# The opening of a two-block transformer kernel: condition, x, modulation tiles and first weights

## The chip, the cores and the metric

The kernel runs on one core of a Trainium2 chip, as one program. The metric is the device time of an execution in microseconds (us); of several runs the median stands. A profile is one execution with the hardware profiler on; its span runs from the first to the last instruction.

## The reference

Two transformer blocks of two layers each work on 256 tokens of 1024 features, in float32. Only the beginning of the first block matters here. A condition vector `c` of 1024 numbers goes through Silu and a matrix of 1024 x 6144 per layer, which gives shifts, scales and gates; the normed tokens are scaled and shifted with them and multiplied by the input weights.

```python
c_act = jax.nn.silu(c)
...
mod = c_act @ w_ada[l] + b_ada[l]
sh1, sc1, gt1, sh2, sc2, gt2 = jnp.split(mod, 6, axis=-1)
h = modulate(rms_norm(x, norm_mix[l]), sh1, sc1)
p = h @ w_in[l]
```

`modulate` is h * (1 + scale) + shift. Behind p come a dilated attention, an RWKV-7 recurrence and a gated MLP, a merge, a convolutional feed-forward network, the second layer, and then the second block.

## The kernel before

Activations lie feature-major: a tensor of 1024 x 256 is eight tiles of 128 x 256 (blocks k = 0 to 7). Every weight matmul is done three times to keep float32 accuracy: `wload` (L125) loads halves of 128 x 1024 float32, ACT casts each to a rounded `hi` (L137), VectorE takes the rest as `lo` (L138), `split` (L195) does the same to activations as `h` and `l` (L201, L202), and `mm3` (L162) multiplies hi by h, hi by l and lo by h (L164 to L166).

The opening, in `build` (L1319), runs in this order of the program. SP's queue loads the identity, the condition as one row `crow`, the eight tiles of x (L1328, 128 KB each), and two pairs of columns of `w_in` (12 and 6, in two halves each). ACT applies Silu to the row; TensorE copies it to all partitions with a matmul of ones, and ACT evacuates that to `cact` (L1344, L1345). `LayerA` (L345) then goes through the 16 modulation tiles of the first 2048 outputs. A tile f is 128 outputs x 1024 inputs, 512 KB. Tiles 0 to 7 make the shifts, 8 to 15 the scales of blocks 0 to 7. They come in pairs of 1 MB, in the order of j = 0, 4, 1, 5, 2, 6, 3, 7 (f = 2j and 2j + 1), the last two pairs in halves; the third weight pair (`late`, columns 10) is loaded ahead of those halves. For each tile VectorE multiplies by `cact` and sums along the row (L371) into one column of `mods`.

`mod_cols` (L389) adds biases and makes `sh` and `am` for two blocks at a time (L396 to L398), so two blocks need four tiles. `modulated` (L412) takes the norm's factor from `rms`: squares on ACT (L215), a running sum on VectorE (L222), matmuls with a column of ones (L228), a root on ACT and a reciprocal (L240, L241), and a spread over all partitions (`spread`, L248). It then multiplies (L418), scales and shifts on ACT (L419), and splits. `mix_a` (L733) starts with `fmulti` (L175): three weight pairs, two columns of outputs each, over the eight blocks, 144 matmuls. The three second columns take banks of a pool of two (`aux`), so one of them waits for an evacuation (L434, L435). The first matmul behind the group is that with the `lora` weights (L467).

A scheduler puts each engine's instructions in order ahead of time, by their place in the program and by when it expects their operands; each engine then keeps its order. `keep_in_program_order` ties an instruction behind the one traced before it on its engine. Eight semaphores go round among the transfers, so an issue waits until the transfer eight places ahead has landed.

Of the kernel before, what the change touches and what calls it, by code (L numbers as in the profile page):

```python
# [17 lines left out]
S = 256  # L18
# [4 lines left out]
C1 = -0.5 * math.exp(-0.5)  # L23
ADA_EVERY = 0.67
PTAPS = 7
FILL = {("f", 0): ((0, 0), (0, 1)), ("f", 1): ((1, 0), (1, 1))}
PBANKS = (4, 2, 2)
PACE = (0.8, 1.5)
# [22 lines left out]
class K:  # L51
    def __init__(self, tc, ctx, ins):
        self.tc, self.nc, self.ins = tc, tc.nc, ins
        E = ctx.enter_context
        self.const = E(tc.tile_pool(name="const", bufs=1))
        self.xp = E(tc.tile_pool(name="xp", bufs=9))
        self.hp = E(tc.tile_pool(name="hp", bufs=17))
        self.wk = E(tc.tile_pool(name="wk", bufs=5))
        self.pm = E(tc.tile_pool(name="pm", bufs=PBANKS[0], space=PSUM))
        self.pa = E(tc.tile_pool(name="pa", bufs=PBANKS[1], space=PSUM))  # L60
        self.pr = E(tc.tile_pool(name="pr", bufs=PBANKS[2], space=PSUM))
        self.dr = E(tc.tile_pool(name="dr", bufs=1, space=DRAM))
        self.n = 0
        self.bg = []
        self.pj = {}
        self.due = 0.0
        self.wps = []
        self.turn = {"raw": 0, "split": 0}
        nc = self.nc
        self.ones = self.const.tile([128, 128], F32, name="ones")  # L70
        nc.vector.memset(self.ones, 1.0 / D)
        self.cols = {}
        self.ca = self.const.tile([128, NCA], F32, name="ca")
# [157 lines left out]
    def rms(self, x, spread=True, tail=False, both=False):  # L231
# [2 lines left out]
        b = self.spread(r, spread)  # L234
        return (r, b) if both else b

    def inv_rms(self, ms):
        nc = self.nc
        r = self.wk.tile([128, 4], F32, tag="st", name=self.nm("rc"), bufs=4)[:, :2]
        nc.scalar.activation(r, ms, AF.Sqrt, bias=self.k(1e-6))  # L240
        nc.vector.reciprocal(r, r)  # L241
        return r
# [83 lines left out]
def v3(t, a):  # L326
    return t.rearrange("p (a b) -> p a b", a=a)
# [14 lines left out]
class LayerA:  # L342


    def __init__(self, G, l, pool, cact, first=None, late=None):  # L345
        nc = G.nc
        self.G, self.l = G, l
        self.pool = p = pool
# [7 lines left out]
        if first is None:  # L356
            self.load_small()
        else:

            for n, j in enumerate((0, 4, 1, 5, 2, 6, 3, 7)):  # L360
                if n == 6:
                    late()
                raw = first.tile([128, 2, D], F32, tag="ada", bufs=8, name=G.nm("raw"))
                src = v3(G.ins["w_ada"][l, j], 2)
                if n < 6:
                    nc.sync.dma_start(raw, src)
                for h in range(2):
                    if n >= 6:
                        nc.sync.dma_start(raw[:, h, :], src[:, h, :])
                    f = 2 * j + h  # L370
                    nc.vector.scalar_tensor_tensor(raw[:, h, :], raw[:, h, :], 1.0, cact, MUL, MUL, accum_out=self.mods[f // 8][:, f % 8:f % 8 + 1])  # L371
        G.bg += [((l, f), ada_task(G, l, f, self.mods, cact)) for f in range(0 if first is None else 16, 48)]

    def load_small(self):
# [36 lines left out]

def modulated(G, x, a, sh):  # L412
    nc = G.nc
    r = G.rms(x, False, True)
    out = []
    for k in range(8):
        t = G.tmp(S)
        nc.vector.tensor_tensor(t, x[k], r, MUL)  # L418
        nc.scalar.activation(t, t, AF.Identity, scale=a[:, k:k + 1], bias=sh[:, k:k + 1])  # L419
        out.append(G.split(t))  # L420
    return out
# [893 lines left out]
def build(tc, ins, outs, stages="AB", depth=DEPTH, dbg=None):  # L1315
    with ExitStack() as ctx:
# [2 lines left out]
        nc = G.nc  # L1319
        G.weights(ctx.enter_context(tc.tile_pool(name="wpa", bufs=1)), 3, 4)  # L1320
        x = []
        G.load_ident()
        LB = nf = sk = pre = None

        def load_x():
            for k in range(8):
                t = G.x1()
                nc.sync.dma_start(t, ins["x"][:, k, :])  # L1328
                x.append(t)
        if "A" in stages:  # L1330
            with tc.tile_pool(name="la", bufs=2) as lp, tc.tile_pool(name="lc", bufs=1) as lc:
# [4 lines left out]
                    pre.append(G.wload(ins["w_in"][0, i], 2048))  # L1336
                with tc.tile_pool(name="st", bufs=1) as sp:
                    G.weights(sp, 3, 2)
                    crow = sp.tile([1, D], F32, name="crow")
                    nc.sync.dma_start(crow, ins["c"])  # L1340
                    nc.scalar.activation(crow, crow, AF.Silu)
                    for i in range(2):
                        ps = G.aux()
                        nc.tensor.matmul(ps, G.ones[0:1, :], crow[:, i * 512:i * 512 + 512], start=True, stop=True)  # L1344
                        nc.scalar.activation(cact[:, i * 512:i * 512 + 512], ps, AF.Copy, scale=float(D))  # L1345
                    load_x()
                    load_w(12)
                    load_w(6)
                    L = [LayerA(G, 0, lp, cact, sp, lambda: load_w(10))]
                    G.wps.pop()  # L1350
                L[0].load_small()
                G.load_consts()
                for l in range(depth):
# [3 lines left out]
                    with tc.tile_pool(name=f"fa{l}", bufs=1) as mp, tc.tile_pool(name=f"wxa{l}", bufs=1) as wx:  # L1357
# [13 lines left out]
                        x = ffn_a(G, L[l], x, l, mp, hook)  # L1371
                        G.wps.pop()
        else:
            load_x()
            G.load_consts()
            with tc.tile_pool(name="la", bufs=1) as lp:
# [129 lines left out]
def arrays(**i):  # L1506
# [2 lines left out]
    out = {"ca": _consts(), "onehot": _onehot()}  # L1509
    out["x"] = _tok(i["x"][0])  # L1510
    out["c"] = i["c"]
    out["w_ada"] = np.ascontiguousarray(i["w_ada"].reshape(L, D, 24, 2, 128).transpose(0, 2, 4, 3, 1)).reshape(L, 24, 128, 2048)
    cw = i["ffn_conv_w"]
    va = [_feat(v) for v in (i["norm_mix"], i["norm_ffn"], i["rwkv_mu"], i["rwkv_w0"], i["rwkv_a0"], i["rwkv_k_k"], i["rwkv_k_a"],
# [59 lines left out]
```

## Time and profile before

| what | value |
|---|---|
| median of 3 runs | 2295.76 us (2294.28 to 2296.1) |
| the profiled execution's own time | 2297.13 us |
| its span | 2295.3 us |
| mean granted TensorE clock | 0.990 |
| TensorE busy | 2206.4 us |
| VectorE (DVE) busy | 1685.2 us |
| ScalarE (ACT) busy | 1286.4 us |
| read from HBM | 408.40 MB |

In the profile PE is TensorE's matmuls and PEld its weight loads, DVE is VectorE, SPq and ACTq are the queues of SyncE and ScalarE. A matmul of plain float32 appears as two records of PE. "L371" is line 371 of the kernel. In brackets stands how long an engine was idle and what ended that.

### The profile page before, as it was taken

Reading aid. Unit: us, or ns where it says so; the run is one execution under the profiler, and the core shown is the slowest. Engines: PE = TensorE matmul, PEld = TensorE weight load, DVE = VectorE, ACT = ScalarE, POOL = GpSimd, SP = SyncE. Lnnn points to the kernel's source line nnn. Section 1 sums busy time; section 2 is a strip of 40 time slices with the busy share of each in tenths; the row PEclk is TensorE's granted clock in tenths of the full one; section 3 lists DMA queues with packets and bytes.
Section 4 is the critical chain, followed back from the end, with each engine's and each line's share of the span. In section 5 each row is a group of like instructions: output and inputs, shape, how many; then the busy total and the mean of one; then the engine's idle time right before and its main releaser. Section 6 shows DMA issues by size and latency. Waiting matters only on the chain.

```text
span 2295.3 us, 46372 instructions
## 1 busy us (share of the span) xinstructions
PE 2206.4 (96%) x18850; PEld 2131.8 (93%) x18850; DVE 1685.2 (73%) x3042; ACT 1286.4 (56%) x2184; POOL 4.2 (0%) x10
## 2 busy tenths in 40 slices
PE   5999998978999999999999999999999999999999
PEld 4889998978888999899999999999999999999999
DVE  6887777757678877776576569976677656997665
ACT  4575546544557554655454466664465446665444
POOL 0000000000000000000000000000000000000000
PEclk9999999989999999999999999999999999999999
DMA  7634457777563446765675663466565556346653
GB/s 289 200 121 150 148 192 256 224 220 231 179 188 122 150 150 190 262 213 156 176 238 170 173 196 109 140 216 184 158 209 182 171 175 194 102 149 214 184 159 124
DMA packets 129148, 416.66 MB, mean 182 GB/s; under 512 B 14596, under 2 KB 20356, under 8 KB 128166
## 3 DMA queue, kind: packets, MB, share of 16 engines
q1 hardware_dynamic: 126750, 409.50, 57.0%
q10 hardware_dynamic: 2184, 4.19, 1.0%
q8 instruction: 148, 2.42, 0.4%
q14 instruction: 66, 0.54, 0.1%
HBM read 408.40 MB, written 5.24 MB: 180 GB/s over the span
## 4 chain that ended last, share of the span: by engine, by line
PE 77%; DMA 9%; DVE 7%; ACT 5%; issue 1%; SPq 0%; ACTq 0%; DVEq 0%
PE ps L164 22%; PE ps L165 22%; PE ps L166 22%; DVE lo L138 3%; DMA skew<-ohb 2%; ACT hi L137 2%; DMA raw<-in_ffn_up 2%; DMA raw<-in_w_ada 2%; DMA raw<-in_w_in 1%; PE rec L601 1%; PE rec L593 1%; DVE raw L371 1%; DMA raw<-in_w_out 1%; PE rec L1182 1%; PE aux L1044 0%
## 5 line engine op out<-in xcount | busy, mean ns | idle before, releaser
L164 PE MATMUL ps<-h,hi 128*128 128x256 f32 x5080 | 1437.1, 284 | 31.0 <-ACT h L201 28.5
L166 PE MATMUL ps<-h,lo 128*128 128x256 f32 x5080 | 1433.2, 283 | 15.4 <-DVE lo L138 15.4
L165 PE MATMUL ps<-l,hi 128*128 128x256 f32 x5080 | 1432.2, 283 | 5.1 <-DVE l L202 5.0
L137 ACT CAST hi<-raw 128x1024 fp32r<-128x1024 f32 (+1 forms) x724 | 704.8, 977 | 640.2 <-PE ps L165 360.3
L138 DVE TENSOR_TENSOR lo<-raw,hi 128x1024 fp32r<-128x1024 f32 (+1 forms) x724 | 819.7, 1134 | 300.7 <-ACT hi L137 297.6
L164 PEld LDWEIGHTS ps<-h,hi 128*128 128x128 f32 x5080 | 959.7, 189 | 44.1 <-ACT h L201 30.8
L166 PEld LDWEIGHTS ps<-h,lo 128*128 128x128 f32 x5080 | 961.2, 189 | 21.0 <-DVE lo L138 16.8
L165 PEld LDWEIGHTS ps<-l,hi 128*128 128x128 f32 x5080 | 961.2, 189 | 11.2 <-DVE l L202 6.8
L201 ACT CAST h<-t 128x256 fp32r<-128x256 f32 x172 | 68.7, 403 | 126.1 <-DVE t L1000 96.2
L202 DVE TENSOR_TENSOR l<-t,h 128x256 fp32r<-128x256 f32 x172 | 72.5, 424 | 66.1 <-ACT h L201 65.7
L338 DVE SCALAR_TENSOR_TENSOR raw<-raw,cact 128x1024 f32<-128x1024 f32 x80 | 97.4, 1218 | 30.3 <-DMA raw<-in_w_ada 30.2
L997 DVE TENSOR_TENSOR t<-ps,r 128x512 f32<-128x512 f32 x88 | 60.8, 691 | 41.6 <-PE ps L166 41.2
L1187 DVE SCALAR_TENSOR_TENSOR cy<-cp,cwh,cy 128x256 f32<-128x256 f32 x192 | 85.2, 478 | 3.2 <-ACT cy L1185 2.9
L215 ACT ACTIVATE t<-x 128x256 f32<-128x256 f32 x96 | 38.5, 407 | 16.4 <-DVE x L968 9.1
L222 DVE TENSOR_TENSOR t<-t,t 128x256 f32<-128x256 f32 x87 | 36.6, 421 | 5.4 <-ACT t L215 4.1
L190 PE MATMUL ps<-hi,h 128*128 128x256 f32 x128 | 38.2, 299 | 0.0
L191 PE MATMUL ps<-hi,l 128*128 128x256 f32 x128 | 37.7, 294 | 0.0
L1000 DVE TENSOR_TENSOR t<-t,t 128x256 f32<-128x256 f32 x88 | 36.9, 420 | 1.0 <-ACT t L999 1.0
L192 PE MATMUL ps<-lo,h 128*128 128x256 f32 x128 | 37.4, 292 | 0.0
L999 ACT ACTIVATE t<-t 128x256 f32<-128x256 f32 x88 | 36.1, 411 | 0.9
L964 ACT ACTIVATE t<-t 128x256 f32<-128x256 f32 x44 | 18.1, 415 | 27.3 <-DVE t L963 27.0
L419 ACT ACTIVATE t<-t,sh,am 128x256 f32<-128x256 f32 x32 | 18.1, 596 | 26.5 <-DVE am L398 22.5
(312 smaller groups left out, 1890.3 us busy)
## 6 DMA issues: line engine op xcount, KB each, us to landing
raw<-in_w_in SPq DMA_DIRECT2D x176, 512.0 KB, 4.3
raw<-in_ffn_in SPq DMA_DIRECT2D x176, 512.0 KB, 4.5
raw<-in_ffn_up SPq DMA_DIRECT2D x88, 512.0 KB, 5.6
raw<-in_w_ada SPq DMA_DIRECT2D x84, 512.0 KB, 4.8
raw<-in_ffn_out SPq DMA_DIRECT2D x64, 384.0 KB, 3.1
raw<-in_ffn_out SPq DMA_DIRECT2D x64, 320.0 KB, 3.2
raw<-in_w_branch SPq DMA_DIRECT2D x24, 512.0 KB, 4.2
raw<-in_ffn_down SPq DMA_DIRECT2D x32, 384.0 KB, 3.1
```

Of the source, the lines that this page charges most:

```text
L137: nc.scalar.copy(hi[:, :m], raw[:, :m])
L138: nc.vector.tensor_tensor(lo[:, :m], raw[:, :m], hi[:, :m], SUB)
L164: mm(ps, w[0], x[0], start=first, stop=False)
L165: mm(ps, w[0], x[1], start=False, stop=False)
L166: mm(ps, w[1], x[0], start=False, stop=last)
L190: mm(ps[:, :256], x[k][0][:, sl], h, start=k == 0, stop=False)
L201: nc.scalar.copy(h, src)
L202: nc.vector.tensor_tensor(l, src, h, SUB)
L215: nc.scalar.square(sq, x[k])
L338: nc.vector.scalar_tensor_tensor(raw, raw, 1.0, cact, MUL, MUL, accum_out=mods[f // 8][:, f % 8:f % 8 + 1])
L997: nc.vector.tensor_tensor(v3(gu, 2), v3(ps, 2), rb, MUL)
L1187: stt(y, cp[:, jj:jj + S], cwh[:, jj * 4 + i:jj * 4 + i + 1], y, MUL, ADD)
```

## The change

The condition goes to all partitions by a broadcast load and gets its Silu there; a second, feature-major copy `cc` (128 x 8) is loaded too. Odd tiles of x are issued on ACT's queue. The sum of squares is done by 16 matmuls of one column over the eight squares, ahead of `LayerA`, and `modulated` takes the result from there. Each modulation tile is a load of 512 KB. Tiles 0, 1, 2, 3 and 5 come from a transposed copy of the weights and are multiplied on TensorE (8 matmuls of one column each, and a copy on ACT); the other 11 stay on VectorE. The tiles come as 8, 0, 9, 1, and so on; the three weight pairs are loaded after the tiles of blocks 1, 3 and 7. The identity is loaded in `rms_pe`.

```diff
+ADA_PE = (0, 1, 2, 3, 5)
...
+    def rms_pe(self, x):
+
+        nc = self.nc
+        ps = self.aux()
+        sqs = []
+        for k in range(8):
+            sq = self.tmp(S)
+            nc.scalar.square(sq, x[k])
+            sqs.append(sq)
+        self.load_ident()
+        for t in range(2):
+            for k, a in enumerate(sqs):
+                nc.tensor.matmul(ps[:, t:t + 1], a[:, t * 128:t * 128 + 128], self.ones[:, 0:1], start=k == 0, stop=k == 7)
+        return self.spread(self.inv_rms(ps[:, :2]), False)
...
-            for n, j in enumerate((0, 4, 1, 5, 2, 6, 3, 7)):
-                if n == 6:
-                    late()
-                raw = first.tile([128, 2, D], F32, tag="ada", bufs=8, name=G.nm("raw"))
...
+            for k in range(8):
+                for f in (8 + k, k):
+                    raw = first.tile([128, D], F32, tag="ada", bufs=16, name=G.nm("raw"))
+                    out = self.mods[f // 8][:, f % 8:f % 8 + 1]
+                    if f in ADA_PE:
+                        nc.sync.dma_start(raw, G.ins["w_ada_pe"][ADA_PE.index(f)])
+                        ps = G.rec()
+                        for i in range(8):
+                            nc.tensor.matmul(ps[:, 0:1], raw[:, i * 128:i * 128 + 128], ccol[:, i:i + 1], start=i == 0, stop=i == 7)
+                        nc.scalar.copy(out, ps[:, 0:1])
+                    else:
+                        nc.sync.dma_start(raw, G.ins["w_ada"][l, f // 2, :, (f % 2) * D:(f % 2) * D + D])
+                        nc.vector.scalar_tensor_tensor(raw, raw, 1.0, cact, MUL, MUL, accum_out=out)
+                late(k)
...
 def modulated(G, x, a, sh):
     nc = G.nc
-    r = G.rms(x, False, True)
+    r = G.first_rms
+    if r is None:
+        r = G.rms(x, False, True)
+    G.first_rms = None
...
-        G.load_ident()
...
-                nc.sync.dma_start(t, ins["x"][:, k, :])
+                G.tc.keep_in_program_order((nc.scalar if k % 2 else nc.sync).dma_start(t, ins["x"][:, k, :]))
...
-                    crow = sp.tile([1, D], F32, name="crow")
-                    nc.sync.dma_start(crow, ins["c"])
-                    nc.scalar.activation(crow, crow, AF.Silu)
-                    for i in range(2):
-                        ps = G.aux()
-                        nc.tensor.matmul(ps, G.ones[0:1, :], crow[:, i * 512:i * 512 + 512], start=True, stop=True)
-                        nc.scalar.activation(cact[:, i * 512:i * 512 + 512], ps, AF.Copy, scale=float(D))
+                    ccol = sp.tile([128, 8], F32, name="ccol")
+                    nc.sync.dma_start(cact, ins["c"].to_broadcast([128, D]))
                     load_x()
-                    load_w(12)
-                    load_w(6)
-                    L = [LayerA(G, 0, lp, cact, sp, lambda: load_w(10))]
+                    G.tc.keep_in_program_order(nc.scalar.dma_start(ccol, ins["cc"]))
+                    nc.scalar.activation(ccol, ccol, AF.Silu)
+                    nc.scalar.activation(cact, cact, AF.Silu)
+
+                    def late(k):
+                        if k in (1, 3, 7):
+                            load_w({1: 12, 3: 6, 7: 10}[k])
+                    G.first_rms = G.rms_pe(x)
+                    L = [LayerA(G, 0, lp, cact, sp, late, ccol)]
```

## Rows read from the trace of the kernel before

**Rows 1.** The page: span, and busy time of the engines

```profile
span 2295.3 us, 46372 instructions
PE 2206.4 (96%) x18850; PEld 2131.8 (93%) x18850; DVE 1685.2 (73%) x3042; ACT 1286.4 (56%) x2184; POOL 4.2 (0%) x10
```

**Rows 2.** Stretches: us, busy PE, PEld, DVE, ACT, POOL, granted clock, DMA share, GB/s

```profile
0.00:5.00 5.00, 1.11 (x2) 0.59 (x3) 0.40 (x4) 3.17 (x4) 1.16 (x5) 1.00 0.43 125
5.00:10.00 5.00, 2.66 (x4) 0.56 (x2) 2.33 (x6) 2.86 (x7) 0.00 (x0) 1.00 0.85 231
10.00:15.00 5.00, 1.87 (x8) 1.78 (x8) 2.45 (x2) 3.93 (x6) 0.00 (x0) 1.00 1.03 394
...
20.00:25.00 5.00, 0.00 (x0) 0.00 (x0) 5.00 (x12) 0.00 (x0) 0.00 (x0) 1.00 1.01 421
```

**Rows 3.** Chain of waits, 15 to 58 us: shares; a piece (start, us, what)

```profile
by line: DVE raw L371 42.6%; DVE lo L138 8.5%; DVE t L418 5.5%; DVE l L202 4.7%; ACT z L434 4.5%; ACT hi L137 4.4%; issue 4.0%; ACT t L419 3.9%; ACT L768 3.0%; PE aux L248 2.9%; PE ps L164 2.0%; PE ps L165 1.4%; PE ps L166 1.4%; PE aux L166
...
20.34 2.29 DVE raw L371 x4
```

**Rows 4.** Waits, 0 to 110 us: us in total, times, longest

```profile
ACT t L419 <- DVE am L398: 22.5, 4, 11.8
```

**Rows 5.** Timeline of SP's queue: start, us, what is issued

```profile
1.56 3.67 SPq L1328 DMA_DIRECT2D x<-in_x  x8
...
25.22 0.33 SPq L369 DMA_DIRECT2D raw<-in_w_ada  x1
```

**Rows 6.** DMA issues at 25 us: count, KB each, us to landing

```profile
raw<-in_w_ada SPq DMA_DIRECT2D x1, 512.0 KB, 14.0
```

**Rows 7.** Timeline of VectorE, end of the modulation tiles

```profile
45.01 1.22 DVE L371 SCALAR_TENSOR_TENSOR raw<-raw,cact 128x1024 f32<-128x1024 f32 x1
...
46.47 0.16 DVE L398 SCALAR_TENSOR_TENSOR am<-am,vec 128x2 f32<-128x2 f32 x1
48.08 0.76 DVE L202 TENSOR_TENSOR l<-t,h 128x256 fp32r<-128x256 f32 x2 [1.45 <-ACT h L201]
```

**Rows 8.** Timeline of TensorE's matmuls in the opening

```profile
10.10 1.87 PE L228 MATMUL aux<-ones,t 128*128 128x1 f32 x8 [2.44 <-ACT cact L1345]
...
30.29 0.58 PE L164 MATMUL ps<-h,hi 128*128 128x256 f32 x1 [13.67 <-ACT h L201]
...
35.30 0.41 PE L165 MATMUL ps<-l,hi 128*128 128x256 f32 x1
35.52 0.41 PE L166 MATMUL ps<-h,lo 128*128 128x256 f32 x1
...
36.36 0.28 PE L164 MATMUL aux<-h,hi 128*128 128x256 f32 x1
36.48 0.28 PE L165 MATMUL ps<-l,hi 128*128 128x256 f32 x1
...
53.17 0.39 PE L164 MATMUL aux<-h,hi 128*128 128x256 f32 x1 [1.26 <-DVE z L435]
...
56.10 1.03 PE L467 MATMUL rec<-z,lora 128*128 128x256 f32 x4
```

**Rows 9.** Timeline of ACT, the first 15 us

```profile
2.78 1.05 ACT L1341 ACTIVATE crow<-crow 1x1024 f32<-1x1024 f32 x1 [0.76 <-DMA crow<-in_c]
...
9.15 0.42 ACT L215 ACTIVATE t<-x 128x256 f32<-128x256 f32 x1 [1.49 <-DMA x<-in_x]
...
11.09 1.04 ACT L137 CAST hi<-raw 128x1024 fp32r<-128x1024 f32 x1 [1.04 <-DMA raw<-in_w_in]
...
14.88 0.26 ACT L240 ACTIVATE rc<-aux,k 128x2 f32<-128x2 f32 x1
```

**Rows 10.** Groups by line and form, VectorE, 10 to 47 us: busy us, mean ns

```profile
L371 DVE SCALAR_TENSOR_TENSOR raw<-raw,cact 128x1024 f32<-128x1024 f32 x16 | 19.0, 1220 | 0.0
L138 DVE TENSOR_TENSOR lo<-raw,hi 128x1024 fp32r<-128x1024 f32 x6 | 7.3, 1222 | 4.7 <-ACT hi L137 4.7
L418 DVE TENSOR_TENSOR t<-x,aux 128x256 f32<-128x256 f32 x8 | 3.1, 415 | 1.3 <-PE aux L248 1.3
```

More of the change, by code (lines that the diff above doesn't have):

```diff
@@ L67, in __init__ @@
         self.wps = []
+        self.first_rms = None
         self.turn = {"raw": 0, "split": 0}
@@ L342, with __init__ @@
 class LayerA:
-    def __init__(self, G, l, pool, cact, first=None, late=None):
+    def __init__(self, G, l, pool, cact, first=None, late=None, ccol=None):
         nc = G.nc
@@ L358, in __init__ @@
         else:
-            for n, j in enumerate((0, 4, 1, 5, 2, 6, 3, 7)):
-                if n == 6:
-                    late()
-                raw = first.tile([128, 2, D], F32, tag="ada", bufs=8, name=G.nm("raw"))
[L364 to L371, printed above, removed]
+            for k in range(8):
[12 more added lines that the diff above has]
+                late(k)
         G.bg += [((l, f), ada_task(G, l, f, self.mods, cact)) for f in range(0 if first is None else 16, 48)]
@@ L1373, in build @@
         else:
+            G.load_ident()
             load_x()
@@ L1511, in arrays @@
     out["c"] = i["c"]
+    out["w_ada_pe"] = np.stack([i["w_ada"][0][:, f * 128:f * 128 + 128].reshape(8, 128, 128).transpose(1, 0, 2).reshape(128, D) for f in ADA_PE])
+    out["cc"] = np.ascontiguousarray(_feat(i["c"][0]))
     out["w_ada"] = np.ascontiguousarray(i["w_ada"].reshape(L, D, 24, 2, 128).transpose(0, 2, 4, 3, 1)).reshape(L, 24, 128, 2048)
```

## The prediction

> **What bounds the kernel now.** TensorE is busy for 96% of the span [rows 1]; nearly all of that is a matmul stream that the change leaves alone. The edit touches the first 60 us, so I read that stretch by itself. The stretch table has TensorE with nothing to do from 20 to 25 us (0.00 of 5) and VectorE full (5.00); the DMA engines are at a share of about 1.0 and some 410 GB/s (394 and 421 in two stretches) from 10 us on, but only at 0.43 and 0.85 in the 10 us before [rows 2]. The opening thus has two full resources. Which ends last? The chain of waits from 15 to 58 us gives 42.6% to line 371, VectorE's product of a modulation tile with the condition, and no large part to a transfer [rows 3]. The waits agree: ACT's modulating line 419 waited 22.5 us, 11.8 of them in one piece, for `am`, which VectorE makes from those sums [rows 4]. The last transfer of a modulation tile was issued at 25.22 us and took 14.0 us [rows 5, 6], so it landed at 39.2; VectorE was through with the tiles at 46.6 (46.47 plus 0.16) [rows 7], 7.4 us behind. VectorE is the bound, and the transfers are the next one behind it. After 46.6 us a tail runs: `h` and `l` of the last two blocks (until 48.84) [rows 7], the rest of the first group of projections, a wait of 1.26 us for the bank that an evacuation frees, 24 last matmuls, and at 56.10 us the first matmul with the `lora` weights [rows 8]. That is my marker: what is behind it hangs on buffers and results that move with it, so I take its shift for that of the whole time.
>
> **The change, part by part.**
>
> *Five tiles off VectorE.* Two products and their two accumulator reads take 2.29 us on the chain [rows 3], so one product costs 1.145 us of VectorE, and five fewer are 5.7 us. All of it is on the path, up to the point where the transfers bind. On TensorE a tile is 8 matmuls of one column. Line 228 has such matmuls: four of them are 8 records in 1.87 us [rows 8]; less the length of the last record that is 0.21 us each, two records a matmul. A tile is 16 records, 3.4 us. TensorE was idle for 13.67 us ahead of the first projection [rows 8], which takes the first tiles. The spacing of 256-column matmuls falls from 0.22 us (35.30 to 35.52) to 0.12 us (36.36 to 36.48) [rows 8]: 256 columns at 1.2 and at 2.4 GHz, though the granted clock reads 1.00 in all of the opening [rows 2]. At the higher clock I put a tile at half, 1.7 us. The five ACT copies of one column (0.26 us for two columns at 14.88 us) [rows 9] lie in ACT's waits for `am` [rows 4]; each is a new wait of ACT for TensorE, with weight casts and modulated blocks queued behind it, which VectorE and TensorE wait for in turn. As TensorE has idle time when these tiles land, I take nothing for it.
>
> *Sum of squares on TensorE.* Six VectorE adds go; VectorE was busy for 2.73 of the first 10 us [rows 2], so that gains nothing. 16 matmuls, 32 records, 6.8 us, take the place of 8 records. Half of them follow the squares as they come, and half, 3.4 us, come behind the last square (done at 9.57 us) [rows 9]: the sum is there at 13 us, against a root at 14.88 us that stood behind two weight casts and a table load on ACT [rows 9]. Cost 0, under the cover of the wait for the first four modulation tiles; without that cover up to 2 us.
>
> *Condition and x.* The row's way over TensorE goes, with two copies; a Silu of 128x1024 comes, whose nearest row is the 1.05 us of the row's own [rows 9]. The broadcast puts 512 KB of traffic at the head of SP's queue: 524 KB at 410 GB/s, 1.28 us. Below, its cost is 0, where it fills time in which the DMA engines wait anyway; above, I take twice its price, 2.6 us, for 128 reads of one row, which no row shows. I take the 1.28, nearest to the rate of all large loads here. SP's eight x issues took 3.67 us [rows 5]; four of them go to ACT's queue, with `cc` behind them, some 2.3 us ahead of ACT's first square. ACT's squares end with the last x now as then. The DMA engines stood idle for 3.6 us of the first 10 (5 x 0.57 and 5 x 0.15) [rows 2]; over 2 of that lie ahead of any landing, so some 1.3 us can be won, which the broadcast spends. Together 0. The identity (64 KB), now behind x on SP's queue, is wanted only after the root: 0.
>
> The Trainium skill ("DMA: Bandwidth & Descriptors", Issuing engines are not separate DMA queues) says that DMAs started by several engines run on the same 16 DMA engines, and that spreading them saves only the time of issuing. By that rule this part is worth four issues, 1.9 us, less the broadcast, and the sum would read 2288.2 instead of 2288.8.
>
> *Order of the weights.* The third weight pair (two loads of 512 KB) was issued ahead of the last four halves of modulation tiles and now comes behind them all; the first two pairs go behind the tiles of two and of four blocks, still ahead of the last tile. The last tile lands 2 x 1.28 = 2.6 us earlier, at 36.7. The tiles come as 16 loads instead of 10: six more issues of 0.33 us [rows 5], while SP waits for transfers anyway. What follows on SP's queue (small tables, the next weights) keeps its place.
>
> *Does VectorE keep up?* Up to the last tile it has 11 products (12.6), four casts (4.9), eight products with the norm (3.1) [rows 10], six `l` (0.38 each, 2.3) and about 18 small column operations of at most 0.16 us [rows 7] (2.8): 25.7 us. The first tile takes the place of the first weight load, which landed at 11.1 us [rows 9]; to 36.7 that is 25.6 us. It just fits, with the transfers as the limit.
>
> *The sum.* Last tile 36.7; its product and columns (45.01 to 46.63, 1.6) [rows 7] end at 38.4; the last `l` 2.2 us later, at 40.6. The third weights land at about 39.2 and are cast (ACT 1.04, VectorE 1.22 each) [rows 9, 10] by 41.7 and 42.9, ahead of need, since the 24 matmuls of the last blocks of the other pairs come first. TensorE then has these and all 48 of the third pair: 72 x 0.118 = 8.5 us, to 49.1. Against 56.1 that is 7.0 us. The tail has grown from 9.5 to 10.7 us, as the third pair lies wholly in it. The profiled execution took 2297.13 us, 1.37 over the median of the runs; less 7.0 it would be 2290.1, and the median **2288.8 us**.
>
> **The rivals.** A difference below 0.2% (4.6 us) is about what a measurement of this kernel can't tell from none: faster means below 2291.2, slower above 2300.4.
>
> *A. TensorE at its lower clock becomes the bound.* From 16.4 us (the sum at 13, one tile) to 40.6 it must do four tiles, the spread of the norm and 72 matmuls: 13.6, 1.2 and 15.3, together 30.1 us at the lower clock and half of that at the higher, in 24.2 us. All at the lower one it is 5.9 us late (2294.7); half of that is likelier, 2291.8. For it: the first projections ran at the low spacing until about 36 us [rows 8]. Against: that was less than 6 us of work, and here TensorE works from the first x on.
>
> *B. The gain is given back behind the marker.* The next weights come behind some 1.5 MB of small tables. If these, not TensorE, set the pace of the second group, 1 to 2 us remain: 2294.5. Against: those loads wait for buffers that the first group frees, and move with it.
>
> *C. The third weights hold up everything (slower).* TensorE takes its work in order. If that order has the third pair's matmuls block by block between the others', as the loop is written, all but the first 12 wait until 41.7 us: 132 x 0.118 = 15.6, 27 of them at the lower clock (2.6 more) and the wait for the bank (1.3) end at 61.2, 5.1 us later than now: 2300.9. It decides once the third pair stands ahead of the second block. Against: before, too, 24 of that pair's matmuls came last, from 53.17 us [rows 8].
>
> *D. The broadcast and the second queue do nothing but cost:* 2.6 us for the one, nothing for the other: 2291.4.
>
> **How the numbers follow.** The forecast with D has 0.62 (its own range 2285 to 2291.5), A 0.16, B 0.12, C 0.10. The low end, 2284, is the forecast with the issue time won, the broadcast for nothing and a tail of the old length, 3.1 us together, and some over. The high end, 2296, takes in A whole and B; C alone is left out. Faster: 0.59 of the first, half of A and little of B, 0.69. Slower: half of C, 0.05. The same: 0.26.
>
> **What would show it.** Right: 11 products on VectorE, the last waiting for its transfer; the last tile landed at 35 to 37 us; the first projection near 22 us instead of 30.3; the marker at 48 to 50. Wrong: a marker beyond 52; one-column matmuls ahead of projections that had all they need; TensorE waiting for a cast of the third weights with other blocks undone; or a marker 7 us early and a span that is not.

## The result, and the profile after

The changed kernel takes 2309.61 us in the median of six runs (2300.36 to 2311.46), the kernel before 2294.60 in the same session (six runs, 2289.37 to 2296.10): a ratio of 1.0063, 95% interval 1.0050 to 1.0077. It is slower by 15 us; 2288.8 was forecast. The profiled execution took 2300.36 us, the fastest of the six, so its end says less than its opening; a second profile of the same kernel (e12 below, 2314.99 us) has the same opening within 0.5 us.

The marker, the first matmul with the `lora` weights, came at 67.32 us instead of 56.10: 11.2 us later. The page, and the stretches of the opening (columns as in [rows 2]):

```profile
span 2298.6 us, 46563 instructions
PE 2222.4 (97%) x18950; PEld 2150.2 (94%) x18950; DVE 1676.8 (73%) x3026; ACT 1286.1 (56%) x2188; POOL 4.2 (0%) x10
```

```profile
10.00:15.00 5.00, 5.00 (x25) 5.00 (x25) 1.53 (x7) 2.65 (x6) 0.00 (x0) 1.00 0.99 370
15.00:20.00 5.00, 5.00 (x24) 5.00 (x25) 1.29 (x3) 0.42 (x2) 0.00 (x0) 1.00 1.00 401
20.00:25.00 5.00, 3.94 (x20) 3.86 (x19) 1.65 (x8) 0.66 (x2) 0.00 (x0) 1.00 1.03 418
...
35.00:40.00 5.00, 3.14 (x15) 3.05 (x15) 0.59 (x2) 2.16 (x5) 0.00 (x0) 1.00 1.04 330
...
50.00:55.00 5.00, 3.56 (x20) 3.36 (x18) 3.60 (x9) 1.26 (x2) 0.00 (x0) 0.72 0.00 0
55.00:60.00 5.00, 4.34 (x22) 4.13 (x23) 3.12 (x4) 2.32 (x5) 0.00 (x0) 0.66 0.34 110
```

Against [rows 2] the engines have changed places: from 10 to 20 us TensorE is full with 49 matmul records, and VectorE, full before from 20 to 25 us, is busy for 1.65 of those 5, and for 0.59 of the 5 from 35. The chain of waits from 15 to 68 us says the same, against 42.6% for VectorE's products in [rows 3]:

```profile
by line: PE rec L385 27.8%; ACT t L441 7.3%; PE ps L168 6.8%; DVE raw L389 6.5%; PE ps L167 6.4%; PE ps L166 5.7%; SPq L912 5.4%; ACT hi L139 5.3%; DMA bsp<-in_b_s 4.9%; PE aux L166 4.1%; PE aux L168 3.8%; PE aux L167 3.4%; PE aux L251 2.4%
```

L385 are the tiles on TensorE: 27.8% of 53 us are 14.7 us on the path. The waits up to 70 us (total, times, longest) show how they get there:

```profile
ACT mod L386 <- PE rec L385: 22.2, 5, 5.5
PE aux L251 <- ACT t L246: 9.3, 1, 9.3
...
DVE sh L415 <- ACT mod L386: 8.5, 3, 5.5
```

ACT stands five times before the one-column copy of a tile. VectorE, which adds the biases to that column, stands behind ACT, and its own landed tiles stand behind VectorE. TensorE's timeline (start, length, what; the bracket is the idle time ahead and what ended it):

```profile
9.28 6.98 PE L251 MATMUL aux<-ones,t 128*128 128x1 f32 x32 [9.28 <-ACT t L246]
16.13 3.55 PE L385 MATMUL rec<-ccol,raw 128*128 128x1 f32 x16
...
20.53 3.41 PE L385 MATMUL rec<-ccol,raw 128*128 128x1 f32 x16
...
26.89 0.58 PE L166 MATMUL ps<-h,hi 128*128 128x256 f32 x1 [2.94 <-ACT h L203]
...
29.91 3.41 PE L385 MATMUL rec<-ccol,raw 128*128 128x1 f32 x16
...
33.17 0.56 PE L167 MATMUL ps<-l,hi 128*128 128x256 f32 x1
...
34.17 3.41 PE L385 MATMUL rec<-ccol,raw 128*128 128x1 f32 x16
...
45.23 1.84 PE L385 MATMUL rec<-ccol,raw 128*128 128x1 f32 x16
...
67.32 1.02 PE L489 MATMUL rec<-z,lora 128*128 128x256 f32 x4
```

The sum of squares ends at 16.26 us instead of 13, the first two tiles at 19.7 and 23.9, the first projection begins at 26.89 instead of near 22, and the fifth tile begins at 45.23, behind projections that had to wait for other tiles. It wasn't late itself: its load was issued at 21.29 us, and these loads took 10.2 us to land (median), so it lay there from about 31.5 on. VectorE's timeline has the longest hole, and the end:

```profile
32.11 0.16 DVE L417 SCALAR_TENSOR_TENSOR am<-am,vec 128x2 f32<-128x2 f32 x1
37.80 0.16 DVE L415 TENSOR_TENSOR sh<-mod,vec 128x2 f32<-128x2 f32 x1 [5.54 <-ACT mod L386]
...
53.54 0.16 DVE L415 TENSOR_TENSOR sh<-mod,vec 128x2 f32<-128x2 f32 x1
55.30 1.23 DVE L140 TENSOR_TENSOR lo<-raw,hi 128x1024 fp32r<-128x1024 f32 x1 [1.60 <-ACT hi L139]
```

The last columns are done at 53.70 us (46.63 before, 38.4 forecast), though the last tile had been issued at 26.40 and landed about 11.2 us later, at 37.6, not far from the forecast (36.7). The transfers kept to the plan; the engines didn't. Of the 11.2 us at the marker, 7.1 are there at the last columns. The other 4.1 come in the tail behind them, which takes 13.6 us instead of 9.5: VectorE waits 1.60 us for the cast of the third weight pair, and the granted clock is 0.66 from 55 to 60 us (before: 1.00 from 45 to 55).

At the head, ACT's timeline:

```profile
0.74 5.03 ACTq L1349 DMA_DIRECT2D x<-in_x  x4
5.80 0.45 ACTq L1363 DMA_DIRECT2D ccol<-in_cc  x1
6.28 1.28 ACT L1365 ACT_TABLE_LOAD   x1 [6.28 <-DMA x<-in_x]
7.57 1.06 ACT L1365 ACTIVATE cact<-cact 128x1024 f32<-128x1024 f32 x1
...
8.83 2.54 ACT L246 ACTIVATE t<-x 128x256 f32<-128x256 f32 x8
```

The five issues held ACT's queue until 6.25 us, with the table load and Silu behind them. The fourth began only at 5.4 us: with eight semaphores in turn it had to wait for the transfer eight places ahead, the broadcast, issued at 0.74 and 4.7 us on its way. The squares ran from 8.83 to 11.37 us, before from 3.89 to 9.57.

### The profile page after: what moved, and what is told of

The parts are those of the page before. It is cut to its first block, busy times and chain, and to the rows that moved or that the text cites. A ratio compares the mean times of both kernels' runs of the same rounds, so it can differ in the third digit from the quotient of the medians.

```text
span 2298.6 us, 46563 instructions
## 1 busy us (share of the span) xinstructions
PE 2222.4 (97%) x18950; PEld 2150.2 (94%) x18950; DVE 1676.8 (73%) x3026; ACT 1286.1 (56%) x2188; POOL 4.2 (0%) x10
## 4 chain that ended last, share of the span: by engine, by line
PE 78%; DMA 9%; DVE 7%; ACT 5%; issue 2%; SPq 0%; ACTq 0%; DVEq 0%
PE ps L166 22%; PE ps L167 22%; PE ps L168 22%; DVE lo L140 3%; DMA raw<-in_w_ada 2%; DMA skew<-ohb 2%; ACT hi L139 2%; DMA raw<-in_ffn_up 2%; DMA raw<-in_w_in 1%; PE rec L623 1%; PE rec L1204 1%; PE rec L615 1%; DMA raw<-in_w_out 1%; PE rec L385 1%; DVE raw L355 1%
## 5 line engine op out<-in xcount | busy, mean ns | idle before, releaser
L355 DVE SCALAR_TENSOR_TENSOR raw<-raw,cact 128x1024 f32<-128x1024 f32 x80 | 97.4, 1217 | 37.6 <-DMA raw<-in_w_ada 37.4
L1021 ACT ACTIVATE t<-t 128x256 f32<-128x256 f32 x88 | 36.3, 412 | 1.5 <-DVE t L1019 0.6
L194 PE MATMUL ps<-lo,h 128*128 128x256 f32 x128 | 36.7, 286 | 0.0
L983 ACT ACTIVATE t<-ps,vec 128x256 f32<-128x256 f32 x44 | 24.5, 559 | 11.8 <-PE ps L168 11.8
```

The lines of the kernel that those rows point to most:

```text
L355: nc.vector.scalar_tensor_tensor(raw, raw, 1.0, cact, MUL, MUL, accum_out=mods[f // 8][:, f % 8:f % 8 + 1])
```

## The experiments

Eighteen kernels ran; the median of before beside them and beside the changed kernel lay between 2293.56 and 2294.60 us. "Last columns" is the end of VectorE's last addition of `sh` or `am`; "full pace" is where TensorE's records first follow each other at the higher clock's spacing (0.11 to 0.12 us instead of 0.21). These columns and the marker are read from one profiled execution each; the two of the changed kernel differ by 0.44 us at the marker.

| kernel | last columns | full pace | marker | median us | ratio (95%) |
|---|---|---|---|---|---|
| before | 46.6 | 36.1 | 56.10 | 2294.60 | |
| changed | 53.7 | 42.6 | 67.32 | 2309.61 | 1.0063 (1.0050, 1.0077) |
| e1_tiles_dve | 44.9 | 32.8 | 57.13 | 2299.41 | 1.0028 (1.0018, 1.0038) |
| e2_norm_dve | 53.6 | 44.2 | 66.02 | 2308.74 | 1.0066 (1.0050, 1.0082) |
| e3_both_dve | 45.1 | 40.4 | 56.42 | 2294.09 | 1.0003 (0.9994, 1.0013) |
| e4_tiles_only | 53.1 | 36.3 | 62.58 | 2300.74 | 1.0039 (1.0022, 1.0055) |
| e5_wide | 42.3 | 12.3 | 54.58 | 2299.47 | 1.0029 (1.0019, 1.0039) |
| e6_copy_dve | 55.5 | 44.6 | 69.33 | 2312.47 | 1.0085 (1.0071, 1.0100) |
| e7_two_tiles | 49.1 | 46.9 | 61.25 | 2309.65 | 1.0069 (1.0054, 1.0084) |
| e8_weights_only | 43.0 | 30.0 | 55.23 | 2294.52 | 1.0014 (1.0000, 1.0029) |
| e9_wide_norm_dve | 47.5 | 21.4 | 59.78 | 2303.08 | 1.0043 (1.0029, 1.0058) |
| e10_before_wide | 46.2 | 21.4 | 55.66 | 2299.06 | 1.0019 (1.0008, 1.0031) |
| e12_after_again | 54.0 | 42.8 | 67.76 | 2310.26 | 1.0069 (1.0056, 1.0081) |
| e13_after_pool | 53.5 | 45.1 | 67.32 | 2308.76 | 1.0065 (1.0050, 1.0080) |
| e14_wide_pool | 43.9 | 13.6 | 57.90 | 2295.27 | 1.0014 (1.0003, 1.0024) |
| e15_wide_norm_pool | 49.7 | 22.9 | 62.13 | 2304.76 | 1.0054 (1.0036, 1.0071) |
| e17_gpsimd | 45.9 | 33.3 | 58.09 | 2297.88 | 1.0023 (1.0012, 1.0033) |
| e18_gpsimd_old | 49.4 | 34.8 | 58.85 | 2298.77 | 1.0022 (1.0012, 1.0031) |

(e11 and e16, the delays, are told below: there the scheduler put other matmuls ahead of the marker.)

### Which part of the change loses

e1 puts the five tiles back on VectorE, e2 the sum of squares, e3 both; e4 gives the kernel before the five tiles on TensorE (with the condition's column, and loads in halves where a pair is split) and nothing else.

```diff
 e1: -ADA_PE = (0, 1, 2, 3, 5)
     +ADA_PE = ()
 e2: -G.first_rms = G.rms_pe(x)
     +G.load_ident()
     +G.first_rms = G.rms(x, False, True)
...
 e4: +if f in ADA_PE:
     +    nc.sync.dma_start(raw[:, h, :], G.ins["w_ada_pe"][ADA_PE.index(f)])
```

> All 16 modulation tiles back on VectorE, the rest as changed. The marker is the first matmul with the lora weights: 56.1 us before, 67.3 us changed. Theory T1 (the five tiles on TensorE are the loss: 3.4 us each in its order, and VectorE waits for their columns with finished transfers' products behind): the marker comes back to 55 to 58 us and the time to within 4 us of before. Rival T2 (the late sum of squares on TensorE is the loss: it ended at 16.1 us instead of 12.0): the marker stays at 63 us or more. Rival T3 (the third weight pair behind all tiles is the loss): the marker stays at 61 us or more, with the last casts of that pair just ahead of it.

> The sum of squares back in the old form (VectorE's running sum, 8 records on TensorE), the tiles still on TensorE. T1: it frees 5 us of TensorE ahead of the first tile, but the waits among the engines remain: marker 62 to 67 us. T2: marker at 60 us or less. T3: no change within 2 us of 67.3.

> Both back: tiles and sum of squares as before; only the condition's broadcast, x over two queues and the order of the weights are left of the change. T1: within 2 us of the run with the tiles alone put back. T2: at least 4 us earlier than that run. T3: marker still over 60 us. If none of the three parts left costs anything, the marker is at 54 to 57 us.

> The kernel before, with the five tiles alone moved to TensorE (order of the loads as before, sum of squares as before). T1: the marker later than before by 4 us or more, VectorE with idle time ahead of its column sums. T2 and T3: the marker earlier than 56.1 us, by up to the 5.7 us of the five products.

Measured: without the tiles the marker falls back to 57.13 us; without the sum of squares it stays at 66.02; without both it is 56.42 and the time that of before. (The time of e1 is 5.7 us over before; within 4 was expected, and its marker is only 1 us late.) The tiles alone, put into the kernel before, delay its marker by 6.5 us. So the tiles on TensorE are the loss; the sum of squares costs about 1 us at the marker (0.7 from e3 to e1, 1.3 from e2 to the changed kernel), not far above the 0.44 by which two executions of one kernel differ. The broadcast, the second queue and the order of the weights together change nothing that can be measured (e3).

### Why the tiles lose: the clock, or the copies

e5 makes each one-column matmul 128 columns wide, with the same column 128 times, and changes nothing else in the program (the sum of squares likewise, against all 128 columns of ones). The scheduler, which goes by expected times, gave some instructions other places in it. e6 leaves the matmuls and puts the copies of the column on VectorE.

```diff
 e5: -matmul(ps[:, 0:1], raw[...], ccol[:, i:i + 1], ...)
     +matmul(ps[:, :128], raw[...], ccol[:, i:i + 1].to_broadcast([128, 128]), ...)
 e6: -nc.scalar.copy(out, ps[:, 0:1])
     +nc.vector.tensor_copy(out, ps[:, 0:1])
```

> The changed kernel with the same matmuls made 128 columns wide (the column of the condition, or of ones, read 128 times; the result is in every column), so that TensorE does more in the same number of records. Theory K (the tiles are dear because TensorE stays at 0.213 us a record all through its one-column matmuls, from 9.3 to 42.5 us): wide ones raise the clock some microseconds after 9.3 us, a tile takes 1.7 to 1.9 us instead of 3.4, and the marker falls by 5 us or more from 67.3. Rival A (it is the waits in ACT's order: casts of weights and modulated blocks stand behind the five copies) and rival V (it is VectorE's order, products behind the columns sh): a spacing that stays at 0.213, or one that falls and a marker that falls by less than 3 us.

> The changed kernel with the five copies of a tile's column on VectorE instead of ACT, so that ACT waits for no tile. A: ACT's casts of the first weights come at 17 to 20 us instead of 25.5 and the marker falls by 4 us or more, to 63 or less. V and K: the marker stays within 2 us of 67.3, since VectorE waits in its order for the same sums.

Measured: the wide matmuls bring the marker from 67.32 to 54.58 us, below that of before; the copies on VectorE make it 2 us worse (VectorE now waits 14.1 us for TensorE itself). Two stretches of the wide kernel, and its last tile:

```profile
9.00:12.00 3.00, 2.73 (x13) 2.73 (x14) 0.53 (x6) 2.98 (x9) 0.00 (x0) 1.00 0.81 253
12.00:14.50 2.50, 2.50 (x22) 2.35 (x21) 1.23 (x2) 0.66 (x1) 0.00 (x0) 1.00 1.01 400
```

```profile
9.27 5.26 PE L251 MATMUL aux<-ones,t 128*128 128x128 f32 x32 [9.27 <-ACT t L246]
14.49 2.05 PE L385 MATMUL rec<-ccol,raw 128*128 128x128 f32 x16
...
35.09 1.95 PE L385 MATMUL rec<-ccol,raw 128*128 128x128 f32 x16
```

13 records in 2.73 us are 0.21 each; 22 in 2.50 are 0.11: the rate doubles at 12.3 us. In the changed kernel 64 one-column records and the four of the norm's spread follow each other from 9.28 to 23.9 us, 0.21 us each, and the doubling comes at 42.6, in the projections. So a record of 128 columns cost no more than one of one column, and in the wide sequence the clock rose, where in the narrow one it did not. The granted-clock column reads 1.00 in both sequences; the spacing of the records tells it.

The 12.7 us between the two kernels are not the pace alone. In e5 ACT makes the first two weight casts ahead of the second tile's copy, in the changed kernel behind both copies; and TensorE has its third tile ahead of the first projection, in the changed kernel behind eight. A cleaner pair is e4 and e10 (below): narrow and wide tiles in the kernel before, with the same order on TensorE (four tiles in a row, 24 projections, the fifth tile). The four tiles, in e4 and then in e10:

```profile
18.54 13.81 PE L375 MATMUL rec<-ccol,raw 128*128 128x1 f32 x64 [1.66 <-DMA raw<-in_w_ada_pe]
```

```profile
18.09 8.96 PE L375 MATMUL rec<-ccol,raw 128*128 128x128 f32 x64 [2.38 <-DMA raw<-in_w_ada_pe]
```

With the pace rising at 21.4 us they take 4.85 us less, the first projection begins at 28.14 us instead of 32.91, and the marker comes at 55.66 instead of 62.58. The granted clock from 40 to 45 us is 0.50 in e4 and 1.00 in e10. Here the width, and with it the pace, makes 6.9 us (ACT and VectorE have a few instructions in other places); how much of the changed kernel's loss is the scheduler's order of the narrow tiles was not measured, since no run holds that order fixed.

The wide kernel is still slower than before as a whole; that is taken up at the end of this part.

### Fewer tiles, and the order of loads alone

e7 has the old sum of squares and only tiles 0 and 1 on TensorE; e8 is the kernel before with the new order of loads (16 loads of 512 KB, the weight pairs behind the tiles of two, four and eight blocks).

```diff
 e7: -ADA_PE = (0, 1, 2, 3, 5)
     +ADA_PE = (0, 1)
 e8: -for n, j in enumerate((0, 4, 1, 5, 2, 6, 3, 7)):
     +for k in range(8):
     +    for f in (8 + k, k):
```

> Sum of squares in the old form, and only tiles 0 and 1 on TensorE, which has nothing else to do when they land (13 to 17 us). If the loss comes from tiles that stand between projections (V, A or K), these two cost nothing and VectorE is free of 2 x 1.145 = 2.3 us: marker 53 to 55.5 us, 1 to 3 us below the run with both parts back (56.4), and the time below before by up to 3 us. If any tile on TensorE costs more than it frees, the marker is at 57 us or more.

> The kernel before with the order of loads alone changed (16 loads of 512 KB in the order 8, 0, 9, 1 and so on, the weight pairs after blocks 1, 3 and 7). The prediction's sum gives it 2.6 us for the last tile's landing, if transfers bind; but with all 16 products on VectorE, VectorE binds: the marker within 1.5 us of 56.1, the time within 0.2% of before. If the third pair at the end costs by itself (T3): the marker 2 us or more later.

Measured: two tiles still cost 5.2 us at the marker, 4.8 over e3, for 2.3 us of VectorE's time saved. This went against every theory by which only tiles between projections cost something: the first two columns hang on TensorE too. The order of loads alone brings the last columns to 42.97 us, 3.66 earlier, but the marker only 0.9 earlier. The tail takes 2.8 of it: the third weight pair's `lo` are made behind the last columns, at 44.57 and 46.32 us, the first after a wait of 1.60 us for ACT's cast, and the last `l` behind them.

### Wide tiles without the sum of squares, and in the kernel before

e9 is the changed kernel with the tiles wide as in e5 and the sum of squares as in e2; e10 is e4 with the same wide tiles; e12 is the changed kernel unaltered. The edit, in e9 and e10:

```diff
-matmul(ps[:, 0:1], raw[...], ccol[:, i:i + 1], ...)
+matmul(ps[:, :128], raw[...], ccol[:, i:i + 1].to_broadcast([128, 128]), ...)
```

> The changed kernel with the five tiles as 128-column matmuls and the sum of squares in its old form (on VectorE, then 8 records). Theory K (one-column matmuls run one behind the other without the clock rising, and that is the loss): the marker comes where the wide kernel had it (54.58 us) or earlier by what the old sum of squares gave with narrow tiles (67.32 to 66.02, so 1.3): 53.3 us, last columns near 41. Theory A (the ACT copies and the order on ACT are the loss): no better than the changed kernel, above 60. Time: if the shift of the marker is carried whole, 2.8 us below before, 2290.8; if the same loss stands behind the marker as in the wide kernel (7.5 us), 2298.

> The kernel before with the five tiles on TensorE as 128-column matmuls, and nothing else of the change (its loads stay in the old order but for the halves; the condition's column is loaded besides). Theory K: VectorE has 5 products less, the last tile still lands near 39, so the last columns come near 42 to 43 and the marker at 51 to 53 (before 56.10, with one-column tiles 62.58). Time if the marker's shift is carried whole: 2289 to 2291. The kernel with one-column tiles and the old order of loads lost only 0.5 us behind the marker, so the theory that the loss behind it comes from the new order of loads says 2289 to 2291 here too; the theory that it comes from any moved stretch of half clock says anything from 2286 to 2297.

> The changed kernel unaltered, for a second profile and more times, since its first profiled execution was the fastest of its six by 8 us. Every theory: marker at 67.3, time 2309 to 2310. If the 11.2 us at the marker are the whole of the loss, the trace ends 11 us after that of before; what it ends later than that is lost behind the marker, and the trace shows where.

e9 missed on both theories' numbers: its marker is 59.78, 5.2 us later than e5, though it has less on TensorE. Its records ran at full pace from 21.4 to 34.3 us, then TensorE waited 1.42 us for an `l`, and the granted clock is 0.50 from 35 to 40 us. TensorE's and VectorE's timelines there:

```profile
38.95 3.29 PE L385 MATMUL rec<-ccol,raw 128*128 128x128 f32 x16
```

```profile
38.76 0.08 DVE L389 DVE_READ_ACCUMULATOR raw<-raw,cact 128x1 f32 x1
42.46 0.16 DVE L415 TENSOR_TENSOR sh<-mod,vec 128x2 f32<-128x2 f32 x1 [3.62 <-ACT mod L386]
```

The last tile stood behind 13 projections at the low pace and took 3.29 us itself; in e5 it ran from 35.09 at the high pace, and VectorE waited 1.05 us for it. That explains 2.6 of the 5.2 us; the rest I can't place. e10 missed as well (marker 51 to 53 expected, and at most 2297 for the time): wide tiles win nothing in the kernel before either (marker 0.4 us earlier for five products fewer, time 4.5 us longer). e12 repeats the changed kernel: marker 67.76, time 2310.26.

### VectorE held in line, and a pure delay

e13, e14 and e15 are the changed kernel, e5 and e9 with the additions of `sh` on GpSimd, so that VectorE doesn't stand there. e11 and e16 add four and eight products on VectorE, into a column that nobody reads, to the kernel before.

```diff
-nc.vector.tensor_tensor(sh[:, c], L.mods[3 * i][:, c], ...)
+(nc.vector if L.l or i else nc.gpsimd).tensor_tensor(sh[:, c], L.mods[3 * i][:, c], ...)
```

> The changed kernel with the four additions that make sh for the first norm on GpSimd instead of VectorE, so that VectorE no longer stands in line for a tile of TensorE. Theory H (VectorE is held in line by TensorE's tiles): its waits for the ACT copies (8.5 us in all, 5.5 in one piece) go, the last product ends at 46 to 49 us instead of 53.5, the marker comes at 61 to 63 instead of 67.3, and the time falls to 2303 to 2306. Theory L (the tiles are late for their own columns whatever VectorE does): the products may end earlier, but the modulating stays late and the marker is within 1.5 us of 67.3, time 2308 to 2311.

> The wide kernel (one-column matmuls made 128 columns) with the same four additions on GpSimd. It had no long wait of VectorE for a copy, so under H nothing is to be won: marker 54 to 55.3 (54.58), time 2298 to 2301. Under L the same. If GpSimd's additions themselves are dear, the marker is later by their price, four times.

> The kernel with wide tiles and the old sum of squares (marker 59.78, VectorE 3.6 us in line for the copy of the last TensorE tile) with the same four additions on GpSimd. H: those 3.6 us go and the marker comes at 55.5 to 57, time 2298 to 2301. L: marker 59 to 60.5, time 2302 to 2304.

Theory H fell. In e13 the marker is the same 67.32 us; the waits up to 60 us show why:

```profile
DVE l L204 <- ACT h L203: 12.2, 3, 7.2
```

VectorE now stands 12.2 us at `l`, one step on, since the blocks themselves can't be modulated before their tile is there: L holds for narrow tiles. In e14 and e15 the marker came 3.3 and 2.4 us later, outside of what either theory said; the same `l` held VectorE 3.3 and 3.5 us in a piece. Yet e14's time, 2295.27, is 4.2 us below e5's (the intervals of the two just overlap). The marker doesn't settle the time.

> The kernel before with four more products on VectorE into a column that nobody reads, behind the last two tiles: a pure delay of 4 x 1.15 = 4.6 us ahead of the marker, with no change of loads, of TensorE's work or of the order behind. If the marker's shift is carried whole: marker 60.7, time 4.6 us over before, 2298.2 (2296.5 to 2300). If what is lost behind the marker is only where the half-clock stretches fall once everything moves, the time is off from that by 3 us or more, either way (2293 or 2303).

> The kernel before with eight more products on VectorE behind the last two tiles, twice the pure delay that cost 2.8 us of 5.4. If a shift at the marker is carried whole: last modulation columns 4.6 us later than there, at 56.7, and the time 4.6 us over it, 2302 (2300 to 2304). If the work behind the marker takes some of a shift in, or adds to it, by where it then falls: off from that by 3 us or more, 2298 or 2306.

Neither was the pure delay it was meant to be: the scheduler put some of the extra products into holes. Their last columns came 5.4 and 2.5 us late, the work from 200 to 250 us (instructions that both traces have) 7.5 and 3.1 us, and the medians are 2.8 and 2.4 us over before. The other way round, from the shift at 200 us to the median: changed kernel 10.5 to 15.0, e7 7.0 to 16.1, e5 0.1 to 5.9, e10 -1.0 to 4.5, but e3 0.3 to 0.4 and e14 2.4 to 1.7. The shift at 200 us is read from one execution, and the second profile of the changed kernel has 14.1 there instead of 10.5. So only differences clearly above 3.6 us say something: e11 lost 4.7 us of its shift, e5, e10 and e7 gained 5.8, 5.5 and 9.1. In these a shift of the opening was not carried to the end as it is.

One piece of this can be read. In e8 the work is 0.9 us early at the marker and 2.9 us late at 200. Its ACT timeline, and below it that of before:

```profile
76.23 1.04 ACT L137 CAST hi<-raw 128x1024 fp32r<-128x1024 f32 x1 [1.94 <-DMA raw<-in_w_in]
77.18 0.25 ACT L531 COPY uv<-rec 64x128 f32<-64x128 f32 x1
```

```profile
75.25 0.26 ACT L537 COPY uv<-rec 64x128 f32<-64x128 f32 x1
...
76.35 1.04 ACT L137 CAST hi<-raw 128x1024 fp32r<-128x1024 f32 x1
```

The scheduler, given other times in the opening, put a weight cast ahead of the `uv` copies; the cast waits for its transfer, TensorE waits 2.2 us for `uv` (0.5 before), and the granted clock is 0.68 from 76 to 80 us and 0.50 from 80 to 84. e5 and e7 have the same wait (1.7 and 2.0 us) and a clock of 0.64 from 76 to 80 and of 0.57 from 84 to 88 respectively. The rest lies mostly between 340 and 420 us (e5 there goes from 1.5 us late at 300 to 5.4 at 400), where all traces have stretches at half clock whose number and place differ, between the two profiles of the changed kernel too. Why some kernels have more of them on the average stays open.

### Would relief of VectorE pay elsewhere

e17 (on e8) and e18 (on before) give tiles 1, 3 and 5 to GpSimd, which multiplies, and ACT, which adds up.

```diff
+if f in (1, 3, 5):
+    nc.gpsimd.tensor_tensor(raw, raw, cact, MUL)
+    nc.scalar.activation(raw, raw, AF.Copy, accum_out=out)
```

> The kernel before with the new order of loads (tiles first, weight pairs behind the tiles of two, four and eight blocks) and tiles 1, 3 and 5 multiplied on GpSimd and added up by ACT instead of both on VectorE. If VectorE is the bound of the opening, as read, three products less are 3.4 us: last columns at 39.5 (order of loads alone: 42.97), marker near 51.8 (55.23), time 3.5 us below that kernel (2294.5) if the shift is carried, 2291. If GpSimd's multiply of 128x1024 takes over 4 us, or slows VectorE beside it, or ACT's additions come late in its order, the marker stays at 55 or later, and the time at 2294 to 2299.

> The kernel before, its loads in the old order, with tiles 1, 3 and 5 multiplied on GpSimd and added up by ACT. If VectorE is the bound, the last columns come 3.4 us earlier at 43.2 (46.62; the last tile lands at 39.2, so transfers don't bind yet), marker 52.7 (56.10), time 2290 to 2291. If GpSimd or ACT's order is too slow for it, marker 56 or later, time 2294 to 2300.

Both lose: markers 2.9 and 2.75 us later than without. GpSimd's and VectorE's timelines in e17:

```profile
24.24 2.90 POOL L366 TENSOR_TENSOR raw<-raw,cact 128x1024 f32<-128x1024 f32 x1 [5.27 <-DMA raw<-in_w_ada]
```

```profile
23.73 1.22 DVE L369 SCALAR_TENSOR_TENSOR raw<-raw,cact 128x1024 f32<-128x1024 f32 x1
...
24.87 3.35 DVE L369 SCALAR_TENSOR_TENSOR raw<-raw,cact 128x1024 f32<-128x1024 f32 x1
```

A product of 1.22 us takes 3.35 when it meets GpSimd's multiply, and ends 1.1 us after it. What VectorE loses to one tile on GpSimd is 2.1 us here, 1.6 at another (a `lo` of 1.22 that took 2.85) and 2.1 at the third (a column operation of 0.16 that took 2.29): 5.9 us together, where the three tiles save it 3.4. The Trainium skill, "SBUF — State Buffer" (Who interferes with whom), says that the two engines share a pair of ports under an exclusive lock; these rows agree. Since VectorE was slowed rather than relieved, these two runs don't show what relief would be worth. No kernel here beats the one before.

## Why the prediction was wrong

**The step that failed** is the costing of the five tiles: "As TensorE has idle time when these tiles land, I take nothing for it", said of ACT's new waits and of TensorE's 3.4 us a tile. The price of a tile was right (3.55, 3.41, and 1.84 us at the higher clock). That it would lie beside other work was wrong: each tile makes a chain of TensorE, ACT's copy, VectorE's addition, ACT's modulating, `h`, `l` and a projection, and the next tile stands behind that projection on TensorE. 14.7 us of tiles lie on the path. The fifth lay landed for some 14 us before TensorE came to it. The prediction held the tiles against the idle time of TensorE ahead of the first projection (13.67 us, and even that is less than five times 3.4) and not against the order in which they stand. e4, with the tiles alone, is 6.5 us late where this part was to gain 5.7. e10, with e4's order on TensorE and the higher clock, comes out level with before at the marker (0.4 us ahead): even there the tiles give back what VectorE was relieved of. Counting that relief at the predicted 5.7, the cost put at nothing was 12.2 us in e4 and 5.3 in e10.

**VectorE keeps up**: "25.7 us" of work was counted for 25.6, and the work was right, but not that VectorE would never wait: 8.5 us at `sh` for ACT's copies, with landed tiles behind. e13 adds that moving that one addition doesn't free it.

**Sum of squares** "at 13 us, cost 0": it came at 16.26. ACT's squares did not end at 9.57 but at 11.37, behind five issues, a table load and Silu, and 4.9 us of the records lay behind the last square instead of half of them, 3.4. TensorE's 32 records (predicted 6.8 us, took 6.98) then held up the first tile: it began at 16.13 us, in e2, without them, at 13.06. As a whole it is about 1 us at the marker.

**Broadcast, second queue**: "Together 0" was right in sum (e3). Not seen was what the two cost ACT: its fourth issue waited until 5.4 us for the broadcast to land, and Silu and the squares stood behind it. The rule weighed there, from the Trainium skill, "DMA: Bandwidth & Descriptors" (Issuing engines are not separate DMA queues), is that a second issuing engine saves only the time of issuing. The runs agree so far that no gain shows: e3 has the second queue and the broadcast, e8 neither, and e3's marker is 1.2 us the later. No run has the second queue alone.

**Order of the weights**: the first half was nearly right (last tile at 37.6, predicted 36.7; first projection at 21.34 in e8, predicted near 22). The tail was undersized: it was to grow to 10.7 us, and takes 12.3 in e8 (42.97 to 55.23) and 13.6 in the changed kernel.

**The rivals.** A named the resource (TensorE at its lower clock), but added up TensorE's work and compared it with the time to the last column, 5.9 us; waits in a chain are not in such a sum, so it stopped at 2294.7, still 1.1 us below before. "Here TensorE works from the first x on" spoke against it and was the error: it worked, and its records stayed at the low pace. D's part holds, in that the broadcast and the queue win nothing, but its sum rests on the tiles like the forecast's. C, the slower one, had another mechanism; the third pair did come last, as argued against it. B expected a gain to be given back behind the marker: there was none to give back, but "a shift of the marker is that of the whole time" did fail, by about 4 us in the changed kernel (11.2 to 15.0, and 11.7 to 15.7 in e12).

**Of what would show it wrong**, the first two signs came: a marker beyond 52, and one-column matmuls ahead of projections that had all they need (at 33.17 us, with an `l` that was made by 30.74, behind the third tile).

## What to carry to other kernels

Before work is moved to an idle engine, write down that engine's order with the moved piece in it, and ask what waits for its result and what it waits behind: five tiles of up to 3.4 us, put into idle time, delayed the marker by 6.5 us where they relieved VectorE of 5.7 (e4), since the columns that everything behind waits for now hung on them. Price work on TensorE at the clock that it will have there, from the spacing of records; here a record of one column was as dear as one of 128, 0.21 us at the lower clock and 0.11 to 0.12 at the higher. And don't take the shift of a milestone for that of the time: the end came here anything from 5 us less to 9 us more than the shift of the work at 200 us. A reordering by the scheduler and stretches at half clock were seen in it; what share each has wasn't measured.

## What the runs showed of the hardware that was not expected

- One-column float32 matmuls with a weight load each, back to back from 9.28 to 23.9 us, ran at 0.213 us a record, the spacing of 1.2 GHz; with 128 columns the sequence that begins at 9.27 us went from 0.21 to 0.11 us a record (2.4 GHz) at 12.3 us. The Trainium skill, "TensorE: Matmul & The Clock Gate" (What's actually happening), has activity release the throttle; the narrow sequence was not followed by a rise until 42.6 us, in the projections, and the wide one was.
- A VectorE product of two SBUF operands took 3.35 us instead of 1.22 beside a GpSimd multiply of 2.90, and a cast's remainder (`lo`) 2.85.
- An engine's own work can stand behind a transfer that it only issues: ACT's fourth issue of x waited for the landing of the broadcast, so that four issues took 5.03 us of its queue (on SP's 1.84), with the table load and Silu behind them.
